# Recurrence of a four-layer hybrid network: both chunks' corrections and the inverse applied ahead of the chain, inverses in blocks of 64, and a scheduler with other prices

## The chip, the cores and the metric

The kernel runs on one core of a Trainium2 chip. Times are device microseconds of one launch; the number that counts is the median of several runs. A trace comes from one more execution, which the hardware profiler records.

## The reference, cut to what matters

A sequence of 512 tokens of width 1024 goes through four layers. Each layer is a mixer and a SwiGLU feed-forward block, each behind an RMS norm and with a residual sum. The mixers are, in this order, an RWKV-7 recurrence, sliding-window attention, a spatial gating unit and gated linear attention. The change is in the first mixer and in the scheduler that orders the whole program. The recurrence of the first mixer has 16 heads with a 64 by 64 state each:

```python
def step(state, inp):
    r_t, d_t, k_t, v_t, kk_t, a_t = inp
    sa = jnp.einsum('bhvk,bhk->bhv', state, kk_t)
    state = (state * d_t[:, :, None, :]
             - sa[..., None] * (kk_t * a_t)[:, :, None, :]
             + v_t[..., None] * k_t[:, :, None, :])
    return state, jnp.einsum('bhvk,bhk->bhv', state, r_t)
```

Its output is normalised per head (mean, variance, reciprocal root), gets a bonus term and a gate, and goes through an output projection `w_o`. All is float32.

## The kernel before

**A recorded program.** The kernel's methods do not issue instructions. Each call (`nc.tensor.matmul` and so on) is recorded as an operation with its reads and writes (`record`), a price in nanoseconds (`price`) and a latency; `Program.run` then lists them. At each turn it takes, over all engines, the operation that could start earliest by the prices, within a window of 700 operations and within the buffers of each pool; an operation that stands earlier in the program is preferred if it would start no more than `SLACK` later than the best. So the order in every engine's queue, in the feed-forward blocks too, follows from the prices. Nearly every instruction has line 233 in the profile, the line at which `run` calls it. Where the planner sees that TensorE would do too little in a stretch of time, `keep_warm` adds dummy products of the identity with itself (line 453 in the profile, `ps<-ident`): their result is not used.

**The recurrence** (`rwkv`) handles the 16 heads as four groups (`n` = 0 to 3) of two head pairs (`i`), and the 512 tokens as 8 chunks of 64, two to a block `b` of 128 tokens. For a group, `ahead(n)` does what needs no state:

- `rwkv_prepare` makes the decayed operands `qk` and `kb` (tiles `h` for even groups, `qk` for odd ones): VectorE scans, exponentials on ScalarE and products on VectorE and GpSimd.
- `rwkv_products` multiplies `kb` with `qk` (TensorE, 64 rows, 128 columns, the two heads of a pair in turn on the two halves of the rows) and masks the result into eight tiles `pa` or `pr`. ScalarE copies the part for the inverse into `z`, one buffer of 16 blocks of 128 by 128 with zeros outside two 64 by 64 blocks on the diagonal.
- `rwkv_inverse` inverts the unit triangular 64 by 64 matrices: blocks of 16 by a substitution of 15 dependent steps on VectorE (tiles `et`), then two levels of doubling on TensorE, four sets `k` of four 128 by 128 blocks each. A level is four transposes, four products with `z`, a masking copy on VectorE (`mt`), four more products and a sum. The result is in four tiles `iv`.

`rwkv_chain` walks over the 8 chunks of a group with the state `st`. One step is: state times `qk` and the correction from the other half of the block (64 by 64 products with `pa` or `pr`) into one bank, a ScalarE copy to `wu`, the 64 by 64 products with the inverse `iv`, a ScalarE copy to `vu`, the products `tok` by `vu`, and on VectorE a product and a sum with the decayed old state (which GpSimd prepares). The chunk's output is four more products per chunk and a copy to `out`. After every second block `rwkv_out` does the normalisation: two reductions and a reciprocal root on VectorE, whose small operations of 128 by 8 elements are `gmean`, `gvar`, `grs` and `rs_t`.

The program stands in the order ahead(0), the value projection, ahead(1), chain(0), ahead(2), chain(1), ahead(3), chain(2), chain(3), then the projection `w_o` for six of the eight operand tiles (`et,rk` on TensorE). Chains of different groups do not depend on each other; what comes next only waits for buffers.

## Time and profile before

| | before |
|---|---|
| median of 3 runs | 2628.28 us (2622.98 to 2630.27) |
| profiled execution, its own time | 2641.05 us |
| its span, first to last instruction | 2639.3 us |
| TensorE busy | 2554.7 us, 97% of the span |
| VectorE, ScalarE, GpSimd busy | 1853.8, 1331.6, 466.0 us |
| mean granted TensorE clock | 0.982 |

The profiled execution is 12.8 us over the median. In the profile, PE is TensorE's matmul stream, PEld its weight loads, DVE VectorE, ACT ScalarE, POOL GpSimd. Names such as `ps<-mt,z` say that a bank `ps` was written from tiles `mt` and `z`, without buffer numbers. A float32 product leaves two matmul records in the trace, a transpose or a float32r product one; so 192 records of `ps<-mt,z` are 96 products. Busy time of matmuls counts their pipeline too, so a group's busy time is more than what it delays others by.

### The profile page before, as it was taken

What the parts mean: (1) busy time and instruction counts of PE and PEld (TensorE: products, weight loads), DVE (VectorE), ACT (ScalarE), POOL (GpSimd) and SP (SyncE); (2) the same over time, 40 slices, a digit from 0 to 9 for tenths busy, and PEclk for the clock granted to TensorE, in tenths of its full rate; (3) what the DMA queues carried; (4) which work ended last, traced back from release to release, by engine and by line L of the source; (5) the groups of instructions that cost most, each with busy time, mean ns of one, the idle gap of its engine ahead of it and who ended that gap; (6) DMA issues with size and microseconds to landing.
All of it is one profiled execution on the core that took longest, in us unless ns stands there. A gap on an engine that the chain in (4) does not pass through costs nothing.

```text
span 2639.3 us, 34990 instructions
## 1 busy us (share of the span) xinstructions
PE 2554.7 (97%) x12974; PEld 2083.4 (79%) x12974; DVE 1853.8 (70%) x2888; ACT 1331.6 (50%) x2208; POOL 466.0 (18%) x492
## 2 busy tenths in 40 slices
PE   8999889999999999999999999999999999999998
PEld 7667767889888775888787888898878777888886
DVE  8675777568787966676868474478777735577868
ACT  3544343356555655655555342365645633555545
POOL 1013333311212234121112000012121000012111
PEclk8989989999999999999999999999999999999999
DMA  3220001148988622499896222379897321389885
GB/s 126 72 68 9 7 7 37 39 126 219 226 215 213 178 84 50 101 223 229 208 227 185 96 96 88 80 176 224 211 228 170 119 96 50 81 221 223 209 209 125
DMA packets 127146, 366.24 MB, mean 139 GB/s; under 512 B 13424, under 2 KB 20976, under 8 KB 126976
## 3 DMA queue, kind: packets, MB, share of 16 engines
q0 software_dynamic: 41472, 138.43, 29.1%
q1 hardware_dynamic: 85504, 225.59, 25.3%
q8 instruction: 102, 1.67, 0.3%
q14 instruction: 68, 0.56, 0.1%
HBM read 359.51 MB, written 2.10 MB: 137 GB/s over the span
## 4 chain that ended last, share of the span: by engine, by line
PE 47%; DMA 5%; issue 5%; DVE 5%; ACT 2%; POOL 0%; SPq 0%; ACTq 0%; POOLq 0%; DVEq 0%
PE ps L233 47%; DMA wraw<-ffn_o_a 2%; DMA wraw<-ffn_w_b 2%; DVE slot L233 2%; DVE wlo L233 1%; ACT whi L233 1%; DVE left L233 1%; DMA wraw<-ffn_w_a 1%; ACT slot L233 1%; POOL wraw L233 0%; DVE h L233 0%; DVE mx L233 0%; DMA wraw<-ffn_o_b 0%; DMA slot<-sg_b_s 0%; DMA slot<-slot 0%
## 5 line engine op out<-in xcount | busy, mean ns | idle before, releaser
L233 PE MATMUL ps<-whi,slot 128*128 128x512 f32 (+1 forms) x5072 | 1548.3, 383 | 14.1 <-DVE slot L233 10.0
L233 PEld LDWEIGHTS ps<-whi,slot 128*128 128x128 f32 x5072 | 942.3, 188 | 190.2 <-issue 22.7
L233 DVE TENSOR_TENSOR wlo<-wraw,whi 128x1024 fp32r<-128x1024 f32 (+2 forms) x628 | 723.1, 1157 | 421.7 <-ACT whi L233 420.5
L233 ACT CAST whi<-wraw 128x1024 fp32r<-128x1024 f32 (+3 forms) x632 | 626.6, 995 | 695.5 <-PE ps L233 528.5
L233 PE MATMUL ps<-wlo,slot 128*128 128x512 f32 (+1 forms) x2536 | 969.3, 382 | 3.7 <-DVE wlo L233 3.6
L233 PEld LDWEIGHTS ps<-wlo,slot 128*128 128x128 f32 x2536 | 476.6, 188 | 87.4 <-DVE wlo L233 7.5
L233 PE MATMUL ps<-slot,whi 128*128 128x512 f32 (+2 forms) x864 | 275.0, 396 | 1.2 <-ACT slot L233 0.9
L233 POOL DMA_DIRECT2D wraw<-ffn_w_a x128 | 109.5, 857 | 502.7 <-DVE wlo L233 363.0
L233 DVE TENSOR_TENSOR slot<-ps,slot 128x512 f32<-128x512 f32 (+2 forms) x287 | 153.3, 566 | 60.4 <-PE ps L233 45.7
L233 PEld LDWEIGHTS ps<-slot,whi 128*128 128x128 f32 (+2 forms) x864 | 156.7, 184 | 48.6 <-issue 9.1
L233 POOL DMA_DIRECT2D wraw<-ffn_w_b x64 | 54.8, 864 | 744.6 <-DMA wraw<-ffn_w_b 505.8
L233 PE MATMUL ps<-slot,wlo 128*128 128x512 f32 (+2 forms) x432 | 169.7, 393 | 0.3 <-DVE wlo L233 0.3
L233 DVE TENSOR_TENSOR slot<-left,slot 128x512 fp32r<-128x512 f32 (+1 forms) x214 | 138.9, 666 | 34.9 <-ACT slot L233 29.1
L233 DVE TENSOR_TENSOR h<-h,ps 128x512 f32<-128x512 f32 x192 | 126.7, 682 | 26.4 <-PE ps L233 25.9
L233 ACT CAST slot<-left 128x512 fp32r<-128x512 f32 (+1 forms) x214 | 124.1, 606 | 31.8 <-PE ps L233 24.7
L233 POOL DMA_DIRECT2D wraw<-ffn_o_a x64 | 54.7, 854 | 278.4 <-DVE wlo L233 162.5
L233 ACT COPY slot<-ps 128x512 f32<-128x512 f32 (+2 forms) x137 | 76.1, 568 | 52.1 <-PE ps L233 51.8
L233 PEld LDWEIGHTS ps<-slot,wlo 128*128 128x128 f32 (+2 forms) x432 | 79.5, 184 | 21.2 <-DVE wlo L233 2.2
L233 PEld LDWEIGHTS ps<-ident,slot 128*128 128x128 f32 x580 | 68.3, 142 | 34.5 <-issue 9.5
L233 PE MATMUL ps<-ident,slot 128*128 128x128 f32 x580 | 89.6, 277 | 3.3 <-POOL slot L233 2.6
L233 ACT COPY left<-ps 128x512 f32<-128x512 f32 x100 | 50.6, 556 | 63.7 <-PE ps L233 63.7
L233 DVE TENSOR_TENSOR slot<-slot 128x512 fp32r<-128x512 f32 (+9 forms) x93 | 61.5, 666 | 18.5 <-ACT slot L233 17.1
(260 smaller groups left out, 2517.3 us busy)
## 6 DMA issues: line engine op xcount, KB each, us to landing
wraw<-ffn_w_a SPq DMA_DIRECT2D x128, 512.0 KB, 6.6
wraw<-ffn_w_a POOLq DMA_DIRECT2D x128, 512.0 KB, 6.0
wraw<-ffn_o_a SPq DMA_DIRECT2D x64, 512.0 KB, 4.8
wraw<-ffn_o_a POOLq DMA_DIRECT2D x64, 512.0 KB, 7.5
wraw<-ffn_w_b SPq DMA_DIRECT2D x64, 384.0 KB, 3.5
wraw<-ffn_w_b POOLq DMA_DIRECT2D x64, 384.0 KB, 6.5
wraw<-ffn_o_b SPq DMA_DIRECT2D x16, 512.0 KB, 5.5
wraw<-ffn_o_b POOLq DMA_DIRECT2D x16, 512.0 KB, 6.1
```

Of the source, the lines that this page charges most:

```text
L233: op = self.add(eng.name, lambda: getattr(eng.target, what)(*map(real, args), **{k: real(a) for k, a in kw.items()}), *self.price(eng.name ...
```

## The change

1. **Chain.** The corrections of both chunks of a block and the products with the inverse are done for the whole block, before the steps, into the bank `xb`; a step then only adds state times `qk`. What the inverse did to `qk` in a step is done once per group by the new `rwkv_direct`: transposes of `qk`, 64 by 64 products with `iv`, and copies back into `qk`. The old state comes into the new one through a product of the identity with `st` in the bank `pb`, in place of a product on GpSimd and a sum on VectorE.
2. **Inverse.** The tiles `pa` and `pr` become one of 4096 columns per group, and the inverse reads its blocks there; `z` and the copies into it go. The sets are two of eight pairs of 64 by 64 blocks, one of each pair in the upper rows and one in the lower, in turn; the transposes there become products with a 64 by 64 piece of the identity.
3. **Normalisation.** The small scalings and the reciprocal root of `rwkv_out` go from VectorE to GpSimd (`rsqrt8`), except for its first operation.
4. **Scheduler.** Prices and latencies change for TensorE, VectorE, ScalarE and GpSimd; a change of the tile size on TensorE is priced at 92 ns, and a 64-row operation after one on the other half of the rows at 0.56 of its price; `SLACK` goes from 60 to 100. `keep_warm` now fills every planned gap of 450 ns or more up to 150 ns before its end, in place of filling up to an activity goal. This holds for the whole program.
5. **Pools.** `et` has 12 buffers for 6, `iv` 4 for 8, and some others one more or less.

```diff
-EARLY = (("pa", 8), ("iv", 8), ("ew", 3))
-LATE = (("qk", 4), ("pr", 8), ("et", 6), ("mt", 6), ("tok", 3), ("wu", 1), ("vu", 3), ("st", 5), ("out", 3), ("gn", 2))
+EARLY = (("pa", 1), ("iv", 4), ("ew", 3))
+LATE = (("qk", 4), ("pr", 1), ("et", 12), ("mt", 6), ("tok", 4), ("wu", 2), ("vu", 4), ("st", 4), ("out", 4), ("gn", 2))
...
-            return max(n * 1.667 + 5.0, m * 1.667, 340.0 if n < 16 and m == P else 0.0), 200.0
+            return max(n * 1.72 + 5.0, m * 1.72, 340.0 if n < 16 and m == P else 0.0), 200.0
...
+                if op.form[:2] != self.form[:2]:
+                    cost += self.TURN
+                elif op.form[0] == 64 and op.form[2] != self.form[2]:
+                    cost *= 0.56
...
+        if not first.done or not free or s - now < self.GAP:
+            return now
+        t = max(now, min(free) + self.SEM)
+        while True:
+            c = 224.0 if work.get(int(t // self.TICK) - 1, 0.0) >= self.BUSY else 448.0
+            if t + c > s - self.TAIL:
+                return now
             call()
...
-        for k in range(4):
-            zk = [z[:, (k * 4 + j) * P:(k * 4 + j + 1) * P] for j in range(4)]
+        halves = [(slice(0, 64), j) for j in range(8)], [(slice(64, P), j) for j in range(8)]
+        blocks = [x for pair in zip(*halves) for x in pair]
+        part = lambda t, r, j: t[r, j * 64:(j + 1) * 64]
+        for k in range(2):
+            zk = lambda r, j: z[r, k * 2048 + j * 256 + (64 if r.start else P):][:, :64]
...
+    def rwkv_direct(self, sb):
...
+        for i in range(2):
+            ps = [self.bank() for _ in range(2)]
+            for bb in range(2):
+                kt, tp = self.part("mt"), self.bank()
+                for j in range(4):
+                    t = (bb * 4 + j) * P
+                    nc.tensor.transpose(tp[:, j * P:(j + 1) * P], sb['qk'][i][:, t:t + P], self.ident)
+                nc.scalar.copy(kt, tp)
+                for b in range(2):
+                    for h in range(2):
+                        for c, ru in ((0, slice(64, P)), (1, slice(0, 64))):
+                            o, j = (b * 2 + c) * P + h * 64, i * 4 + h * 2 + b
+                            nc.tensor.matmul(ps[c][h * 64:(h + 1) * 64, (bb * 2 + b) * 64:(bb * 2 + b + 1) * 64], kt[ru, o:o + 64],
+                                             sb['inv'][bb][ru, j * 64:(j + 1) * 64], start=True, stop=True)
...
+            ab, xb = self.bank(), self.bank()
+            for i, h in heads:
+                for c, (rv, ru) in enumerate(halves):
+                    mm(ab[ru, hc(i, h)], pc(i, h, c, 1 - c)[rv], sb['v'][b][rv, hc(i, h)], start=i + h == 0, stop=True)
+            w1 = self.part("wu", w=W)
+            nc.scalar.copy(w1, ab[:, :W])
+            for i, h in heads:
+                for c, (rv, ru) in enumerate(halves):
+                    mm(xb[:, c * W:(c + 1) * W][ru, hc(i, h)], inv(i, h)[ru], w1[ru, hc(i, h)], start=i + h == 0, stop=False)
...
-                    if st is not None:
-                        nc.vector.tensor_add(ns, ns, sp)
+                        for i in range(G):
+                            mm(pb[:, col(i)], self.ident, st[:, col(i)], start=i == 0, stop=False)
...
-        nc.vector.tensor_scalar(var, var, 1.0 / 64, 64e-5, op0=ALU.mult, op1=ALU.add)
-        self.rsqrt(rs, var)
+        nc.gpsimd.tensor_mul(var, var, self.k8['mean'])
+        nc.gpsimd.tensor_add(var, var, self.k8['eps'])
+        self.rsqrt8(rs, var)
```

Three places show what this does to TensorE's queue. The first is the inverse of one group (tiles `mt`) as its first doubling level starts, with steps of another group's chain between. Before:

```order
L453 MATMUL ps<-ident 128x128 x10
L233 MATMUL ps<-ident,mt 128x128 x4
L233 MATMUL ps<-mt,z 128x128 x4
L233 MATMUL ps<-st,qk 128x128
L233 MATMUL ps<-ident,mt 128x128 x4
L233 MATMUL ps<-st,qk 128x128
L233 MATMUL ps<-mt 128x128 x4
L233 MATMUL ps<-vu,pr 64x64 x4
```

Now, in the last group:

```order
L448 MATMUL ps<-ident 128x128 x54
L233 MATMUL ps<-st,ident 128x128 x2
L233 MATMUL ps<-st,h 128x128 x2
L448 MATMUL ps<-ident 128x128
L233 MATMUL ps<-ident,mt 64x64 x16
L233 MATMUL ps<-vu,tok 128x128
L233 MATMUL ps<-mt,pr 64x64 x16
```

Runs of four operations of 128 by 128 have become runs of sixteen of 64 by 64, and the dummy products (`ps<-ident` with line 448) stand in one long run ahead of them.

The second place is a step of the chain of an odd group on TensorE, from one `st,qk` (state times `qk`) to the next. Before, with the next group's products (`qk`) between:

```order
L233 MATMUL ps<-st,qk 128x128 x2
L233 MATMUL ps<-vu,pr 64x64 x4
L233 MATMUL ps<-qk 128x128 x3
L233 MATMUL ps<-wu,iv 64x64 x4
L233 MATMUL ps<-qk 128x128 x3
L233 MATMUL ps<-vu,tok 128x128 x2
L233 MATMUL ps<-vu,pr 64x64 x4
```

Now:

```order
L233 MATMUL ps<-st,ident 128x128 x2
L233 MATMUL ps<-st,qk 128x128 x2
L233 MATMUL ps<-g_1282,tg 128x256
L233 MATMUL ps<-wu,iv 64x64
L233 MATMUL ps<-vu,tok 128x128 x2
L233 MATMUL ps<-vu,pr 64x64 x4
```

Between the state's product and `vu,tok` no 64 by 64 product of the same step is left (the `wu,iv` is one for a later block); the product `st,ident` is new.

The third place is the middle of the last feed-forward block, where TensorE multiplies split weights (`whi`, `wlo`) with split operands (`slot`). Before:

```order
L233 MATMUL ps<-wlo,slot 128x512
L233 MATMUL ps<-whi,slot 128x512 x3
L233 MATMUL ps<-wlo,slot 128x512
L233 MATMUL ps<-whi,slot 128x512 x2
L233 MATMUL ps<-wlo,slot 128x512
```

Now:

```order
L233 MATMUL ps<-wlo,slot 128x512
L233 MATMUL ps<-whi,slot 128x512 x5
L448 MATMUL ps<-ident 128x128 x12
L233 MATMUL ps<-wlo,slot 128x512
L233 MATMUL ps<-whi,slot 128x512 x2
```

The products are the same; twelve dummy products now stand between two of them. In the whole program there are 399 dummy products for 160: 62 for 35 before the recurrence, 142 for 98 in it up to the last group's outputs, and 195 for 27 behind it.

More of the change, by code (lines that the diff above doesn't have):

```diff
@@ L178 @@
 class Op:
-    __slots__ = ("i", "eng", "call", "deps", "outs", "wait", "cost", "lat", "table", "bufs", "ready", "end", "done", "columns")
+    __slots__ = ("i", "eng", "call", "deps", "outs", "wait", "cost", "lat", "table", "bufs", "ready", "end", "done", "columns", "form")
 class Engine:
@@ L298, in run @@
         dma, table, work = 0.0, None, {}
-        self.work, self.near = work, {}
+        self.work = work
         avail = {e: [] for e in now}
@@ L1261, in rwkv_chain @@
[L1261 to L1268 removed]
+                        mm(x[:, col(i)], sb['qk'][i][:, col(b * 2 + c)], st[:, col(i)], start=False, stop=False)
@@ L1319, in rwkv_out, with rsqrt8 @@
             self.split(ps[:, i * W:(i + 1) * W], sb['oo'][i][0][:, hf * W:(hf + 1) * W], sb['oo'][i][1][:, hf * W:(hf + 1) * W])
+    def rsqrt8(self, y, x):
+        nc = self.nc
+        t = self.sm.tile([P, 8], F32, name="rs8")
+        nc.vector.tensor_scalar(y.bitcast(I32), x.bitcast(I32), -0.5, float(0x5f3759df), op0=ALU.mult, op1=ALU.add)
+        nc.gpsimd.tensor_mul(x, x, self.k8['half'])
+        for _ in range(3):
+            nc.gpsimd.tensor_mul(t, y, y)
+            nc.gpsimd.tensor_mul(t, t, x)
+            nc.gpsimd.tensor_add(t, t, self.k8['one5'])
+            nc.gpsimd.tensor_mul(y, y, t)
     def row(self, ap, n=S):
```

166 lines of the change are left out of this document (73 added, 93 removed).

## The prediction

> **What bounds the kernel now.** I read the page first, then the busy times by stage, then who waits for whom on TensorE, then the groups of the recurrence's stretch.
>
> ```profile
> PE 2554.7 (97%) x12974; PEld 2083.4 (79%) x12974; DVE 1853.8 (70%) x2888; ACT 1331.6 (50%) x2208; POOL 466.0 (18%) x492
> 0.00:132.00 132.00, 123.03 (x513) 90.31 (x514) 99.75 (x162) 64.25 (x96) 10.74 (x11) 0.95 0.29 99
> 132.00:553.00 421.00, 384.23 (x2760) 317.22 (x2760) 291.50 (x569) 174.39 (x362) 131.65 (x128) 0.91 0.09 30
> 553.00:2640.00 2087.00, 2047.40 (x9704) 1675.86 (x9702) 1462.53 (x2159) 1092.97 (x1751) 323.58 (x354) 1.00 0.65 163
> ```
>
> After each stretch stand the busy microseconds of PE, PEld, DVE, ACT and POOL, then the granted TensorE clock. PE is busy for 97% of the span, so it bounds everything. But the recurrence, 132 to 553, is the one stretch where PE is not only busy: its clock averages 0.91, and the records of dummy products stand there most densely:
>
> ```profile
> 132.00:553.00 421.00, 35.84 (x196) 27.98 (x196) 0.91 0.09 30
> 553.00:2640.00 2087.00, 8.10 (x54) 7.89 (x54) 1.00 0.65 163
> ```
>
> These are the records of the dummies alone: 98 dummies in the recurrence, 27 behind it. The clock is either full or half here, so 0.91 of 421 us means about 76 us at half speed, which cost up to 38 us. Where it happens shows finer:
>
> ```profile
> 157.00:177.60 20.60, 19.84 (x80) 12.85 (x81) 10.25 (x15) 5.02 (x15) 1.32 (x1) 0.50 0.08 26
> 256.00:300.00 44.00, 36.37 (x240) 30.13 (x240) 34.99 (x72) 12.99 (x29) 18.46 (x17) 0.77 0.04 10
> 350.00:390.00 40.00, 34.13 (x212) 29.45 (x213) 28.33 (x58) 14.47 (x27) 18.78 (x18) 0.70 0.03 7
> 430.00:460.00 30.00, 24.95 (x189) 21.67 (x189) 27.41 (x56) 9.46 (x22) 17.41 (x17) 0.90 0.20 67
> ```
>
> From 157 to 177.6 PE was busy 19.84 of 20.6 us, all at half clock: about 10 us lost there alone. The other three are the times in which VectorE makes the next group's operands and substitutions; from 430 to 460 it is busy 27.41 of 30. Who PE waits for in the recurrence says the same:
>
> ```profile
> PE ps L233 <- DVE et L233: 9.9, 6, 3.5
> PE ps L233 <- DVE mt L233: 8.6, 4, 4.4
> PE ps L233 <- POOL mt L233: 3.9, 4, 2.5
> PE ps L233 <- DVE h L233: 3.7, 1, 3.7
> ...
> PE ps L233 <- DVE st L233: 1.2, 1, 1.2
> PE ps L233 <- ACT wu L233: 1.1, 3, 0.6
> ...
> PE ps L233 <- ACT vu L233: 0.5, 1, 0.5
> ```
>
> All 13 rows of that answer add up to 35.6 us. The chain's own links (`st`, `wu`, `vu`) are 2.8 of it; 26.1 belong to what runs ahead of the chain (`et`, `mt`, `h`). So a shorter step is worth little by itself; a lighter VectorE and a shorter inverse are worth more.
>
> **The change part by part.** *TensorE's work.* Prices come from back-to-back runs:
>
> ```profile
> 306.81 0.61 PE L233 MATMUL ps<-mt,z 128*128 128x128 f32 x4
> 307.26 0.61 PE L233 MATMUL ps<-mt 128*128 128x128 f32 x4
> ...
> 439.98 0.67 PE L233 MATMUL ps<-wu,iv 64*64 64x64 f32 x8
> ...
> 440.59 0.71 PE L453 MATMUL ps<-ident 128*128 128x128 f32 x4
> ...
> 246.58 2.05 PE L233 MATMUL ps<-qk 64*128 64x128 f32 x24
> 249.35 1.16 PE L233 MATMUL ps<-qk 64*128 64x128 f32 x8 [0.72 <-DVE pr L233]
> ```
>
> Two products of 128 by 128 (4 records) take 307.26 - 306.81 = 0.45 us, 0.225 each; a transpose, one record, about 0.11. Four 64 by 64 products (8 records) take 440.59 - 439.98 = 0.61 us with a change of the tile size at each end; without those changes (about 0.07 us each) 0.12 each. Taken away: 256 products and 128 transposes of the inverse, 57.6 + 14.1 = 71.7 us. Added: 48 products `st,ident`, 10.8 us, 64 transposes in the new direct form, 7.0 us, and 1152 products of 64 by 64 for 256. What one of those costs is the open price. The last two rows bound it: they are the products of `kb` and `qk`, 64 rows each, the first run mostly on the two row halves in turn, the second on one half. Four products took 1.16 us, 0.29 each; of the 12 in the first run the last four stand on one half too, so the first eight took at most 2.05 - 1.16 = 0.89 us, 0.11 each, half of a full product's 0.225. In the new order nearly all 64 by 64 products stand in turn on the two halves. At half price (0.06) the 1152 cost 69.1 us, at full price 138.2, against 30.7 for the 256: net with the rest -15.5 us or +53.6. I take **-12**, near the first, for the row with alternating halves is the nearest one, and some products stay alone.
>
> That the change counts on such pairs is where a rule speaks against it. The Trainium skill, "TensorEngine Tiling (Array Packing)", Restrictions and Gotchas, says under Gotcha 1 that different row tiles cannot access the same PSUM bank at once. In the `qk` rows the two heads go to two banks; the new pairs go to one bank, on different partitions. No run here shows 64-row pairs in one bank; by that rule the sum would take the +53.6.
>
> *The clock.* Up to 38 us were lost. The new filler puts dummies into every planned gap of 450 ns, 142 in the recurrence for 98, 13 of them ahead of the first group's operands, where the 10 us above were lost. Ends: 0 and -38; I take **-22**, the losses where PE was busy most (10 us at 157, most of the 12 from 350 to 390, where 0.70 of 40 us is 24 at half).
>
> *The waits ahead of the chain.* VectorE loses, by these rows:
>
> ```profile
> L233 DVE TENSOR_TENSOR mt<-ps,mk 128x512 f32<-128x512 f32 x24 | 16.5, 688 | 15.7 <-PE ps L233 15.4
> L233 DVE TENSOR_TENSOR st<-st 128x256 f32<-128x256 f32 x24 | 13.1, 545 | 0.4
> L233 DVE SCALAR_TENSOR_TENSOR rs_t<-gvar,rs_t 128x8 f32<-128x8 f32 x24 | 6.5, 271 | 0.6
> L233 POOL TENSOR_TENSOR mt<-et,mk 128x512 f32<-128x512 f32 x12 | 20.4, 1730 | 4.8 <-DVE rs_t L233 3.8 <-DVE gmean L233 1.1
> L233 POOL TENSOR_TENSOR st<-st,pend 128x256 f32<-128x256 f32 x24 | 16.7, 695 | 16.8 <-DVE st L233 9.9 <-PE ps L233 4.8 <-DVE rs_t L233 1.6
> ```
>
> Half of the inverse's 64 masks and sums, 32 x 0.688 = 22 us; the 24 sums into the state, 13.1; 88 small operations of the normalisation at about 0.27, 24: together 59 of its 291.5 us. GpSimd loses 24 products with the old state, 16.7 us, and half of 16 masks at 1.73, 13.8; it gains 128 operations of 128 by 8. No row has such an operation on GpSimd. The nearest are its 128x256 at 0.695 us from above, at most 89 us, and nothing from below. The cost grows with the elements (1.73 for 512 with the same kind), so I take 0.15 each, 19 us: GpSimd's 131.65 us of 421 leave room. What queues behind them is `out<-out,gn` and the masks `mt`, which TensorE waited 3.9 us for. The ends for the waits: -36 us if all go, +10 if none goes and the 44 more dummies (44 x 0.225) stand on top. I take **-16**: the substitution of 15 dependent steps stays and the shorter chain leaves PE less to do beside it; this is what is late next, and where the run of 54 dummies stands.
>
> *Behind the recurrence.* Nothing is computed otherwise, but 195 dummies stand there for 27: 168 x 0.225 = 37.8 us. They cost nothing where PE waits anyway. How much it waits there:
>
> ```profile
> PE ps L233 <- DVE slot L233: 15.0, 28, 1.5
> PE ps L233 <- DVE h L233: 5.6, 7, 1.7
> ...
> PE ps L233 <- DVE rcol L233: 0.9, 2, 0.6
> ```
>
> The seven rows add up to 28.4 us, so at least 9 us are not covered, and at most 38. At the place of the last feed-forward block that gets 12 dummies PE does not wait at all:
>
> ```profile
> 2605.57 0.84 PE L233 MATMUL ps<-whi,slot 128*128 128x512 f32 x3
> 2606.25 0.39 PE L233 MATMUL ps<-wlo,slot 128*128 128x512 f32 x1
> ```
>
> The next product starts 0.68 us after three at 0.227. I take **+22**, a bit under the middle of the two ends, for the attention stage's waits are at places with dummies. The 27 more at the start stand where PE waits for the first loads: nothing, hidden by that wait, at worst 6 us.
>
> *The sum.* -12 - 22 - 16 + 22 = -28 us. The profiled execution took 2641.05 us, 12.8 over the median of 2628.28; I take the difference over: **2600 us**.
>
> **The rivals.** *More comes free* (2566): the waits go as VectorE's 59 us would allow and most dummies behind the recurrence fall into waits: -15 - 30 - 29 + 12 = -62. For it speaks how closely PE's waits follow VectorE; against it, that the substitution is a chain.
>
> *The pairs do not overlap* (2666): the 64 by 64 products of one bank run one after the other. Then the first term is +53.6, and the rest stays: +53.6 - 22 - 16 + 22 = +38 us, slower. The place is the inverse, 768 of the products; it decides from about 0.084 us each on (28 us over 1152 above 0.06). Against it are the eight `qk` products at 0.11; for it, that those wrote two banks. This is the rule named above, as a mechanism of this kernel.
>
> *Waits become dummies* (2632): the substitution of the next group bounds the recurrence as before, so PE's waits are only filled, and all dummies behind it delay real work: -12 - 22 + 0 + 38 = +4 us. This is also the case in which the change does not do what it says: steps get shorter, but no step was waited for. For it speak the 2.8 us of the chain's links; against it, VectorE's lighter load.
>
> **How the numbers follow.** My forecast 0.50, more comes free 0.17, no overlap 0.18, waits become dummies 0.15. The forecast's own range is 2578 to 2622; with the rivals I give 2562 to 2660, which leaves out the far halves of two of them. About 0.3%, 8 us, is what a measurement of this kernel can tell from no change. Faster (under 2620.4): 0.46 of the forecast's half and the 0.17, 0.63. Within: 0.03 and 0.10, 0.13. Slower: 0.18 of the no-overlap case, 0.05 of the dummies and 0.01, 0.24.
>
> **What would show it.** In the new profile, a run of 16 products `ps<-mt` of 64 by 64 takes about 1.1 us with its tail where the pairs overlap, 2 us where not. The clock of the recurrence is above 0.96. The recurrence (from the first `twa` product to the last `ident,out`) is about 50 us shorter than 421. Behind it, PE's waits are smaller and the stretch is about 22 us longer than 2087. VectorE's busy time falls by about 59 us. I am wrong if the 64 by 64 runs take full price, if the new stretch behind grows by 35 us or more, or if PE's waits for `mt` and `et` are as long as before.

## The result: 1% slower

| | before | changed |
|---|---|---|
| median | 2626.46 us (4 runs, 2622.98 to 2630.27) | 2652.23 us (4 runs, 2650.05 to 2656.64) |
| ratio | | 1.0100, 95% interval 1.0078 to 1.0121 |
| profiled execution | 2641.05 us | 2654.14 us |
| TensorE, VectorE, GpSimd busy | 2554.7, 1853.8, 466.0 us | 2591.7, 1816.0, 454.9 us |

The forecast was 2600 us. The time lies inside the range, but on the other side of no change. The page's first line of the changed kernel already warns against reading busy time as progress, for TensorE is busier by 37 us:

```profile
PE 2591.7 (98%) x14764; PEld 2130.5 (80%) x14764; DVE 1816.0 (68%) x2744; ACT 1317.6 (50%) x2143; POOL 454.9 (17%) x591
```

The first profile of before was an unlucky execution, 15 us over its median. A second one of the same kernel took 2626.73 us, and it is the one to compare with. The stage windows of the changed kernel follow, cut where the recurrence's last output has been split (`rk`, 537.2 us), then the same two stretches for the dummies alone:

```profile
132.00:537.20 405.20, 376.99 (x4168) 313.36 (x4167) 239.68 (x429) 153.34 (x299) 130.78 (x228) 0.91 0.12 39
537.20:2652.40 2115.20, 2088.91 (x10028) 1722.66 (x10027) 1473.80 (x2156) 1100.13 (x1748) 313.42 (x351) 1.00 0.65 160
```

```profile
132.00:537.20 405.20, 37.28 (x284) 34.94 (x284) 0.91 0.12 39
537.20:2652.40 2115.20, 60.35 (x390) 54.79 (x390) 1.00 0.65 160
```

And the second profile of before, cut at the same operation (544.5 us):

```profile
132.00:544.50 412.50, 374.83 (x2794) 312.14 (x2793) 293.94 (x573) 175.95 (x365) 132.87 (x128) 0.95 0.10 33
544.50:2625.00 2080.50, 2043.66 (x9671) 1672.60 (x9669) 1460.35 (x2156) 1090.74 (x1748) 322.28 (x353) 1.00 0.66 163
```

The recurrence gained 7.3 us where about 50 were forecast. The stretch behind it lost 34.7 us where 22 were. Together that is +27.4, the difference of the two spans. (Some 3 us of each only changed sides: float32r products that stood in the recurrence before and stand outside it now.)

To see what the gap between two windows is made of, each matmul's time to the next one's start was split: up to its own length at full clock it is work, what half speed adds to that is clock, and the rest is a gap (short up to 0.35 us, a wait above). Behind the recurrence, some 12 us after the last product are in no row. Sums in microseconds:

| | recurrence, before | changed | behind, before | changed |
|---|---|---|---|---|
| other float32 products and transposes | 165.9 | 115.1 | 158.8 | 159.3 |
| products of 64 by 64 | 29.8 | 68.3 | | |
| float32r products | 83.0 | 79.6 | 1803.6 | 1806.2 |
| dummies | 21.6 | 31.5 | 5.8 | 41.1 |
| half clock | 15.1 | 27.4 | 0.7 | 3.1 |
| short gaps | 56.0 | 52.6 | 69.6 | 78.6 |
| waits | 41.1 | 30.8 | 30.7 | 14.7 |

Two things stand out. In the recurrence, waits and dummies together are 62.7 us before and 62.3 after: what left the waits went into dummies. Behind it, they went from 36.5 to 55.8. The waits of TensorE as the trace names them, first in the recurrence (all 11 rows: 27.7 us against 36.5 in the second profile of before), then behind it:

```profile
PE ps L233 <- DVE out L233: 8.1, 5, 2.6
PE ps L233 <- DVE iv L233: 4.7, 2, 2.8
PE ps L233 <- DVE h L233: 3.5, 2, 2.6
PE ps L448 <- DVE st L233: 3.2, 2, 2.3
PE ps L233 <- DVE mt L233: 3.1, 2, 2.5
```

```profile
PE ps L233 <- DVE slot L233: 6.7, 23, 1.2
PE ps L233 <- ACT slot L233: 2.4, 3, 1.3
PE ps L233 <- ACT whi L233: 1.6, 3, 0.7
```

Behind the recurrence the row for `slot` has gone from 12.8 us in the second profile of before (15.0 in the first) to 6.7 while the stretch became longer. A shorter wait is no gain when a dummy stands in its place.

### The profile page after: what moved, and what is told of

The parts are those of the page before. It is cut to its first block, busy times and chain, and to the rows that moved or that the text cites. A ratio compares the mean times of both kernels' runs of the same rounds, so it can differ in the third digit from the quotient of the medians.

```text
span 2652.4 us, 38408 instructions
## 1 busy us (share of the span) xinstructions
PE 2591.7 (98%) x14764; PEld 2130.5 (80%) x14764; DVE 1816.0 (68%) x2744; ACT 1317.6 (50%) x2143; POOL 454.9 (17%) x591
## 4 chain that ended last, share of the span: by engine, by line
PE 69%; DMA 4%; issue 4%; DVE 2%; ACT 1%; POOL 1%; ACTq 0%; POOLq 0%; DVEq 0%
PE ps L233 67%; PE ps L448 2%; DMA wraw<-ffn_o_a 1%; DMA wraw<-ffn_w_a 1%; DVE slot L233 1%; ACT whi L233 1%; DMA wraw<-ffn_w_b 1%; DVE wlo L233 1%; POOL wraw L233 0%; DMA wraw<-ffn_o_b 0%; DVE mx L233 0%; ACT slot L233 0%; POOL out L233 0%; DVE h L233 0%; POOL rs L233 0%
## 5 line engine op out<-in xcount | busy, mean ns | idle before, releaser
L233 ACT CAST whi<-wraw 128x1024 fp32r<-128x1024 f32 (+2 forms) x632 | 626.0, 993 | 739.0 <-PE ps L233 570.7
L233 DVE TENSOR_TENSOR h<-h,ps 128x512 f32<-128x512 f32 x192 | 128.4, 684 | 30.8 <-PE ps L233 29.1
L233 DVE TENSOR_TENSOR slot<-left,slot 128x512 fp32r<-128x512 f32 x214 | 136.4, 656 | 13.9 <-ACT slot L233 9.5
L448 PE MATMUL ps<-ident 128*128 128x128 f32 x798 | 115.5, 291 | 7.0 <-DVE st L233 3.2
L448 PEld LDWEIGHTS ps<-ident 128*128 128x128 f32 x798 | 107.3, 197 | 16.6 <-PE ps L448 4.9
L233 ACT COPY slot<-ps 128x512 f32<-128x512 f32 (+1 forms) x137 | 75.5, 561 | 80.6 <-PE ps L233 79.6
L233 PEld LDWEIGHTS ps<-ident,slot 128*128 128x128 f32 (+1 forms) x676 | 70.6, 141 | 25.3 <-issue 7.5
L233 PE MATMUL ps<-ident,slot 128*128 128x128 f32 (+1 forms) x676 | 88.2, 265 | 1.0 <-DVE slot L233 1.0
```

The source lines that it names most:

```text
L233: op = self.add(eng.name, lambda: getattr(eng.target, what)(*map(real, args), **{k: real(a) for k, a in kw.items()}), *self.price(eng.name ...
L448: self.nc.tensor.target.matmul(self.ps.tile_pool.tile([P, S], F32, name="ps")[:, :P], self.ident.real(), self.ident.real(), start=True, st ...
```

## The experiments

Eighteen runs followed. "Ratio" is to the kernel before, run beside each on the same chip; the changed kernel is 1.0100. The kernel before stood at medians of 2624 to 2628 us there, so medians of two rows can differ by some 4 us for that alone; the ratios do not have this error.

| run | median us | ratio, interval |
|---|---|---|
| no dummies behind | 2650.21 | 1.0095 (1.0070 to 1.0119) |
| old scheduler behind | 2620.23 | 0.9984 (0.9967 to 1.0001) |
| old prices of three engines behind | 2636.86 | 1.0035 (1.0013 to 1.0057) |
| old scheduler behind, slack 100 | 2621.19 | 0.9977 (0.9959 to 0.9995) |
| the same with TensorE's new prices behind | 2640.65 | 1.0046 (1.0027 to 1.0064) |
| old filler everywhere | 2664.53 | 1.0141 (1.0119 to 1.0164) |
| new scheduler alone | 2683.48 | 1.0227 (1.0201 to 1.0254) |
| new recurrence alone | 2652.01 | 1.0095 (1.0064 to 1.0126) |
| before, again | 2626.73 | (one run) |
| 3 of 15 steps | 2628.51 | 1.0014 (1.0000 to 1.0028) |
| tile in two halves | 2655.66 | 1.0124 (1.0107 to 1.0141) |
| old scheduler behind, dummies in the first wait | 2616.89 | 0.9965 (0.9943 to 0.9987) |
| old scheduler behind, root on VectorE | 2604.64 | 0.9921 (0.9894 to 0.9948) |
| both of these | 2597.87 | 0.9876 (0.9839 to 0.9914) |
| root on VectorE alone | 2635.66 | 1.0028 (1.0011 to 1.0045) |
| old prices of three engines everywhere | 2626.56 | 1.0004 (0.9988 to 1.0021) |
| old scheduler behind, root on VectorE, old prices | 2612.78 | 0.9941 (0.9917 to 0.9966) |
| pairs apart | 2729.33 | 1.0383 (1.0350 to 1.0416) |

### Behind the recurrence: the dummies, or the order?

The first theory was the forecast's own: dummies delay real work. The first run takes them out behind the recurrence.

```diff
-            if e == "PE" and self.warm and op.ready > 0.0:
+            if e == "PE" and self.warm and op.ready > 0.0 and op.i < self.stop:
...
+        nc.stop = len(nc.ops)
         self.load_h()
         self.rwkv_out_proj(oo, 0, 6)
```

> The changed kernel with no dummy products behind the recurrence (195 go; the 62 at the start and the 142 in the recurrence stay). Theory A, dummies delay real work: the stretch behind the recurrence grew by 33 us (from 2082 to 2115), and 195 dummies by 0.225 us are 44 us; without them most of the 33 come back, about 2652 - 30 = 2622 us. Rival B, the new prices put the products there in a worse order and the dummies only fill waits: the time stays within 8 us of 2652, and TensorE's waits behind the recurrence rise by the dummies' time.

Measured 2650.21 us: nothing came back. Theory A fell. This is where TensorE waited behind the recurrence, without a dummy there:

```profile
PE ps L233 <- DVE wlo L233: 15.6, 19, 2.2
PE ps L233 <- DVE slot L233: 12.3, 20, 1.8
PE ps L233 <- POOL slot L233: 5.7, 2, 3.1
PE ps L233 <- DVE h L233: 4.9, 3, 2.5
```

By the split above the waits rose to 53.9 us, in the place of 41.1 of dummies and 14.7 of waits; half clock took 13.5 for 3.1. The dummies had stood in waits that the order itself makes. Those are not the waits of before: `wlo` was 3.1 us in its second profile. So the order was next, by giving the operations behind the recurrence the old prices, slack and filler.

```diff
+        op = self.add(..., *(self.price_old if self.stop else self.price)(eng.name, what, args, kw))
...
+                    if floor is None or s < floor - (60.0 if op.i >= self.stop else self.SLACK):
...
+                now["PE"] = (self.keep_warm_old if op.i >= self.stop else self.keep_warm)(now["PE"], s, work)
...
+                if op.i >= self.stop:
+                    pass
+                elif op.form[:2] != self.form[:2]:
```

> The changed kernel, in which prices, slack and filler go back to those of before for every operation recorded behind the recurrence; the recurrence is scheduled as in the change. Theory D (the new prices put the products behind the recurrence in an order with more waiting, and dummies only fill that): the 22 us that the program lost behind its first 660 us come back, about 2630 us. Rival (the loss behind has another cause, such as the recurrence handing over later loads): within 8 us of 2652.

Measured 2620.23 us: 32 us came back, the whole loss and a little more. Three runs divide it. In the first only VectorE's, ScalarE's and GpSimd's prices go back:

```diff
+        op = self.add(..., *(self.price_old if self.stop and eng.name != "PE" else self.price)(eng.name, what, args, kw))
```

> The changed kernel, in which only the prices of VectorE, ScalarE and GpSimd go back to those of before for operations behind the recurrence; the slack of 100, TensorE's new prices and the new filler stay. 34 dummies are left behind the recurrence for 195. Theory P (the new prices book an operation's duration, 0.685 us of a VectorE sum of 128 by 512, where back to back they start every 0.602 us; the planner sees waits that are none and orders the products by them): the 30 us behind come back, 2618 to 2628 us. Rival (the slack or the filler did it): 2640 us or more.

Measured 2636.86: about half (15 us). The second has the old scheduler behind, as in the run before last, but keeps the new slack; its edit is shown against that run:

```diff
-                    if floor is None or s < floor - (60.0 if op.i >= self.stop else self.SLACK):
+                    if floor is None or s < floor - self.SLACK:
```

> The kernel with the old scheduler behind the recurrence (2620 us), but with the slack of 100 there in place of 60; prices and filler behind stay those of before. Old prices alone behind brought back 15 of 32 us (2637). If the slack is the other half: 2632 to 2640 us. If it is TensorE's price of a tile-size turn or the filler: 2620 us within 5.

Measured 2621.19: the slack costs nothing. The third adds TensorE's new prices to that:

```diff
-        op = self.add(..., *(self.price_old if self.stop else self.price)(eng.name, what, args, kw))
+        op = self.add(..., *(self.price_old if self.stop and eng.name != "PE" else self.price)(eng.name, what, args, kw))
...
-                if op.i >= self.stop:
-                    pass
-                elif op.form[:2] != self.form[:2]:
+                if op.form[:2] != self.form[:2]:
```

> The kernel with old prices and filler and a slack of 100 behind the recurrence (2621 us), but with TensorE's new prices there: 1.72 ns per column, 92 ns for a change of the tile size, 0.56 for a second product of 64 rows. 60 dummies behind for 31. If these prices are the half of the loss behind that the prices of the other engines left (2637 with the new filler): 2630 to 2640 us. If not, 2621 us within 5, and what is left lies with the new filler's places.

Measured 2640.65, 19 us over the run before it, with intervals far apart. So both sets of prices cost, 15 to 19 us each, in a stretch in which nothing is computed otherwise. From the old scheduler behind to the new one, the five medians form a ladder: the slack adds 1 us (2620 to 2621), TensorE's prices 19 (2641), the new filler takes 4 off (2637), and the prices of the other three engines add 15 (2652). The slack and the filler are within the error, so the two sets of prices make up the loss. Which of TensorE's three prices does it was not tried.

Why prices that look better make a worse order can be read in part. The new ones are close to what a record of the trace lasts: 681 ns for a VectorE operation on two inputs (TENSOR_TENSOR) of 128 by 512, 584 ns for a ScalarE copy of that size out of a bank. The changed kernel's group row for a sum of that kind has a mean of 684 ns, but of two in a row the second does not wait that long; the next two rows are two such operations and two copies back to back:

```profile
L233 DVE TENSOR_TENSOR h<-h,ps 128x512 f32<-128x512 f32 x192 | 128.4, 684 | 30.8 <-PE ps L233 29.1
```

```profile
583.23 1.28 DVE L233 TENSOR_TENSOR slot<-left,slot 128x512 fp32r<-128x512 f32 x2
```

```profile
694.81 1.07 ACT L233 COPY left<-ps 128x512 f32<-128x512 f32 x2 [1.97 <-PE ps L233]
```

The two operations take 1.28 us, so the second starts 1.28 - 0.68 = 0.60 us after the first; the old price is 601 ns. Two copies take 1.07, with 0.59 for one they start 0.48 apart; the old price is 476 ns. The old prices are the time an operation keeps its engine, with the rest as latency; the new ones book the whole duration as time in use. That this is how the planner comes to waits that are none is argued; that these prices cost 15 us behind the recurrence is shown.

The old filler under the new prices shows the other side:

```diff
-        if not first.done or not free or s - now < self.GAP:
-            return now
-        t = max(now, min(free) + self.SEM)
...
+        t, free = max(now, s - 2 * self.TICK), pool.slots["ps"].free
+        goal = self.LEVEL * self.BUSY / self.PARTS
```

> The changed kernel with the filler of before (up to an activity goal), everything else as changed: 34 dummies at the start, 83 in the recurrence for 142, 134 behind it for 195. Theory A: 61 fewer behind and 59 fewer in the recurrence, 27 us at 0.225 us each, of which a part was filled waiting: 2627 to 2640 us. Theory B: 2652 within 8 us. If the new filler's dummies in the recurrence had kept the clock up, its share at half speed (71.6 us in both traces) would rise here.

Measured 2664.53, slower than both theories said. Fewer dummies (251 for 399) were worse: with these prices the waits are there, and unfilled they cost some clock too. The times at half speed in the recurrence are 78.5 us for 70.5, and half clock cost 8.5 us behind it for 3.1.

### The recurrence and the scheduler, each alone

For the scheduler alone, the class that lists the operations was taken over into the kernel before, and nothing else; for the recurrence alone, the reverse.

```diff
-            return 68.0 + n * (0.52 if fast else 1.042) + 61.0 * columns, 130.0
+            return 148.0 + n * (0.52 if fast else 2.1 if what == "tensor_tensor_scan" else 1.042) + 61.0 * columns, 60.0
...
```

> The kernel before with the new scheduler alone (prices, slack, tile-size turn, new filler); recurrence as before. 419 dummies for 160: 170 behind the recurrence for 33, 187 in it for 92. Theory A: 137 more behind at 0.225 us are 31 us, most of it uncovered, and 95 more in the recurrence (21 us) partly: about 2626 + 25 to 45 = 2650 to 2670 us. Rival C, the loss comes from the recurrence's new form: about 2626 us.

```diff
-                if op.form[:2] != self.form[:2]:
-                    cost += self.TURN
-                elif op.form[0] == 64 and op.form[2] != self.form[2]:
-                    cost *= 0.56
...
```

> The new recurrence, inverse, normalisation and pools with the scheduler of before (old prices, slack 60, old filler). 28 dummies behind the recurrence, 155 in it, and 400 changes of the tile size on TensorE in the recurrence for 264. Theory A: nothing is lost behind; the recurrence keeps the 20 us that it gained, less some 12 us for the changes of the tile size (136 by about 0.09 us): 2606 to 2618 us. Rival C: 2640 us or more. If the new prices are what makes the new recurrence pay, it comes out at 2626 or above by a longer recurrence.

The scheduler alone took 2683.48 us, worse than either theory's range (waits and dummies in its recurrence, split as above, are 80.7 us for 62.7); the recurrence alone 2652.01, as bad as both together. The two parts need each other: with the new scheduler in the recurrence and the old one behind it, the same recurrence stood at 2620. The trace of the recurrence alone shows short gaps of 72.8 us there for 52.6, and waits and dummies of 73.4 for 62.3, though 13 us of float32r products moved out of it. TensorE's price of a tile-size change, without which the new recurrence has 399 such changes for 264, may be what it lacks. That price was not tried by itself, neither here nor behind the recurrence.

### Before once more, and the clock

> The kernel before, unchanged, for a second profile: the first profiled execution took 2641.05 us, 15 us over the median of its runs (2626). If that came from the clock's windows in the recurrence, this profile shows less than the 71.6 us at half speed there and its recurrence is shorter than 425 us; the new recurrence then gained less than the 20 us that the two profiles show. If not, both stretches are within 5 us of the first profile's.

It took 2626.73 us with the same code. The recurrence was 412.5 us for 425.1, and the stretch behind 2080.5 for 2082.2; the times at half speed in the recurrence sum to 37.5 us for 71.7. Nearly all of the difference is the clock: half speed cost 26.5 us of the first and 15.1 of the second, and some 7 of these 11 us lie in one place. This is 156 to 186 us of the changed kernel, of the second profile of before, and of the kernel below with dummies in the first wait:

```profile
156.00:186.00 30.00, 26.45 (x106) 19.23 (x106) 18.47 (x33) 6.31 (x9) 2.61 (x2) 0.60 0.05 18
```

```profile
156.00:186.00 30.00, 28.50 (x149) 21.01 (x150) 25.25 (x50) 12.38 (x27) 2.04 (x2) 0.94 0.20 65
```

```profile
156.00:186.00 30.00, 29.04 (x169) 21.70 (x168) 25.67 (x54) 12.15 (x18) 1.26 (x1) 1.00 0.06 19
```

TensorE works at 0.60 of its clock here in the changed kernel, behind a wait of 2.58 us for VectorE's operands:

```profile
155.74 0.33 PE L233 MATMUL ps<-ident,h 128*128 128x128 f32 x1
158.65 0.90 PE L233 MATMUL ps<-h 64*128 64x128 f32 x6 [2.58 <-DVE h L233]
```

The filler put five dummies at 150 us and none here: the plan had no gap at this place that it could fill. The next kernel puts twelve in by hand.

```diff
+            if op is self.lead and self.warm[0].slots["ps"].free:
+                for _ in range(12):
+                    self.warm[1]()
+                    self.fills += 1
             op.call()
```

> The kernel with the old scheduler behind the recurrence (2620 us), and 12 dummy products put by hand ahead of the first group's products of 64 rows, into the 2.6 us for which TensorE waits for VectorE there. In the changed kernel and all its variants with the new prices a stretch of 20 to 24 us at half clock begins right behind that wait (at 157 to 162 us). Theory K (the wait makes the clock fall): the stretch shrinks to under 7 us and the time falls by 7 to 12 us, to 2608 to 2613 us. Rival (the products of 64 rows themselves are too little activity): the clock falls all the same, 2620 us or, with 2.7 us of dummies, up to 3 more.

```profile
154.42 2.84 PE L511 MATMUL ps<-ident 128*128 128x128 f32 x24
157.20 0.93 PE L234 MATMUL ps<-h 64*128 64x128 f32 x6
```

In its profile the clock stayed full here, and half speed cost the recurrence 14.5 us for 25.6 in the kernel without these dummies. The same holds for the one other kernel that has them (the last one of the next section). Of the eighteen profiles in which TensorE waits here unfilled, 2.57 to 3.72 us, fifteen show 13.7 to 23.9 us at half speed right behind the wait. The other three show less: 6.8 us with the new recurrence alone, 3.4 in the second profile of before, none with the new scheduler alone. So the wait brings the half clock in most executions, not in each, and the dummies keep it away in the two profiled. Over all executions the mean granted clock agrees: 0.987 with the dummies for 0.984 without (ten each). The median, 2616.89, is 3 us lower, with overlapping intervals, so the gain in time is not settled by these runs.

### What holds the recurrence up

Dummies stand most densely in three stretches, those of the substitution's 15 steps on VectorE. The rows are of the dummies alone, in the changed kernel:

```profile
278.00:300.00 22.00, 11.41 (x84) 11.05 (x84) 1.00 0.01 1
350.00:362.00 12.00, 4.97 (x38) 4.59 (x38) 1.00 0.00 1
420.00:434.00 14.00, 11.37 (x101) 11.37 (x101) 1.00 0.44 143
```

One run cuts the steps; the other frees the masked products' tile in halves.

```diff
-        for i in range(1, 16):
+        for i in range(1, 4):
```

> The changed kernel with 3 of the 15 substitution steps on VectorE; it leaves out 12 steps of each group, about 10.8 us of dependent work per group. Theory S (TensorE waits, or is filled with dummies, for the substitution): 51 dummies in the recurrence for 142, and 25 to 40 us less: 2612 to 2627 us. Rival T (what bounds the recurrence is that the products of group n+2 need the one buffer that the chain of group n still reads): the next groups' products still start when a chain ends; the gain is at most the last two groups' parts, under 15 us: 2637 us or more.

```diff
-EARLY = (("pa", 1), ("iv", 4), ("ew", 3))
+EARLY = (("pa", 2), ("iv", 4), ("ew", 3))
...
-        if hf == 0:
-            sb['pr'] = self.part("pr" if sb['n'] % 2 else "pa", w=8 * S)
+        pr = self.part("pr" if sb['n'] % 2 else "pa", w=4 * S)
+        sb.setdefault('pr', []).append(pr)
```

> The changed kernel with the tile of masked products (4096 columns per group, one buffer) split into two tiles of 2048 with two buffers in the same space, so that half of it comes free when the chain of the group before last is half done; the substitution's first step is done in 8 pieces for 4. Theory T: the products of the third and fourth group start up to half a chain (15 to 30 us) sooner and the recurrence loses 10 to 20 us: 2632 to 2642 us. Theory S: within 8 us of 2652.

With three steps 2628.51 us, 24 us less, and 51 dummies for 142. That is what theory S said, a little short of its range: while VectorE substitutes, TensorE has too little else to do. It is not all that holds the recurrence up. Of the 26 us that the recurrence lost in this trace (379.2 for 405.2), 12 are waits and dummies, 50 us being left of 62, and 9 are half clock. The steps left out also took 36 us of work off VectorE (239.7 to 203.4), and the run cannot tell that from their length as a chain.

With two halves 2655.66, no gain, but the products did not start sooner either. The third group's first masking operation starts at 329.03 us for 325.29, the fourth's at 408.04 for 407.84. So this buffer is not what holds them, and theory T falls as far as it names the buffer. What earlier products would be worth is not shown.

The other candidate is the normalisation. VectorE's waits in the changed kernel, second row:

```profile
DVE st L233 <- PE ps L233: 31.1, 14, 3.2
DVE out L233 <- POOL grs L233: 18.0, 8, 3.5
```

VectorE stood 18.0 us for GpSimd's reciprocal root, a wait that cannot be in the kernel before, where VectorE makes the root itself. Everything behind `out` in VectorE's queue stood with it. The first half of one root on GpSimd, from the last block, and what VectorE does from the sum for the variance to the scaled output:

```profile
525.94 0.20 POOL L233 TENSOR_TENSOR gvar<-gvar,k8half 128x8 f32<-128x8 f32 x1 [0.28 <-DVE grs L233]
526.10 0.20 POOL L233 TENSOR_TENSOR rs<-grs 128x8 f32<-128x8 f32 x1
526.38 0.53 POOL L233 TENSOR_TENSOR rs<-rs,gvar 128x8 f32<-128x8 f32 x1
526.99 0.53 POOL L233 TENSOR_TENSOR rs<-rs,k8one 128x8 f32<-128x8 f32 x1
527.59 0.53 POOL L233 TENSOR_TENSOR grs<-grs,rs 128x8 f32<-128x8 f32 x1
528.20 0.20 POOL L233 TENSOR_TENSOR rs<-grs 128x8 f32<-128x8 f32 x1
```

```profile
524.41 0.69 DVE L233 TENSOR_REDUCE gvar<-out 128x8 f32<-128x512 f32 x1 [0.31 <-ACT out L233]
525.69 0.17 DVE L233 TENSOR_SCALAR grs<-gvar 128x8 int32<-128x8 int32 x1 [0.59 <-POOL gvar L233]
526.14 1.93 DVE L233 TENSOR_TENSOR et<-et 128x512 fp32r<-128x512 f32 x3 [0.28 <-PE ps L233]
530.39 0.69 DVE L233 TENSOR_TENSOR out<-out,grs 128x512 f32<-128x512 f32 x1 [2.32 <-POOL grs L233]
```

From the variance (its sum ends at 524.41 + 0.69 = 525.10) to the scaled output at 530.39 are 5.3 us. Two runs put the root and the small scalings back, one beside the old scheduler behind, one alone:

```diff
-        nc.gpsimd.tensor_mul(mean, mean, self.k8['mean'])
+        nc.vector.tensor_scalar(mean, mean, 1.0 / 64, None, op0=ALU.mult)
...
-        nc.gpsimd.tensor_mul(var, var, self.k8['mean'])
-        nc.gpsimd.tensor_add(var, var, self.k8['eps'])
-        self.rsqrt8(rs, var)
+        nc.vector.tensor_scalar(var, var, 1.0 / 64, 64e-5, op0=ALU.mult, op1=ALU.add)
+        self.rsqrt(rs, var)
```

> The kernel with the old scheduler behind the recurrence (2620 us), with the normalisation's small operations and reciprocal root back on VectorE. The trace of the change shows them at 0.20 to 0.53 us each on GpSimd, 5.3 us from the variance to the scaled output in the last block, against 3.2 on VectorE before. If they were a bottleneck on GpSimd: 3 to 8 us faster, 2612 to 2617. If VectorE's load was worth taking off: 5 to 15 us slower, 2625 to 2635 us.

> The changed kernel with one part undone: the normalisation's small operations and the reciprocal root back on VectorE; the new scheduler everywhere. If GpSimd's place for the root costs by itself what it cost beside the old scheduler (16 us): 2636 us within 6. If it was luck of the plan there: 2652 us within 6.

Measured 2604.64 and 2635.66: 16 and 17 us less than without that edit, in both settings. That is more than the 3 to 8 expected at first, and what the second run expected. TensorE shows where it comes from: in the second run's trace its waits and dummies in the recurrence are 47 us for 62, and its wait for `out` is 3.6 us for 8.1. On VectorE the same stretch of the last block is 2.3 us, from 497.35 to 499.61:

```profile
496.68 0.67 DVE L234 TENSOR_REDUCE gvar<-out 128x8 f32<-128x512 f32 x1
497.39 0.17 DVE L234 TENSOR_SCALAR gvar<-gvar 128x8 f32<-128x8 f32 x1
...
499.61 0.69 DVE L234 TENSOR_TENSOR out<-out,grs 128x512 f32<-128x512 f32 x1
```

VectorE's busy time in the recurrence is 249.5 us with the root and 238.2 without it: moving it saved 11 us of work and added 17.0 of waiting (18.0 in the changed kernel).

Two more runs ask whether the new prices of VectorE, ScalarE and GpSimd are worth having in the recurrence.

```diff
+        op = self.add(..., *(self.price_old if eng.name != "PE" else self.price)(eng.name, what, args, kw))
```

> The changed kernel with the prices of before for VectorE, ScalarE and GpSimd in the whole program; TensorE's new prices with the tile-size turn, the slack of 100 and the new filler stay. 62 dummies in the recurrence for 142, 34 behind for 195. Theory P: the recurrence gains as well, since its planned waits shrink too: 2595 to 2615 us. Rival (the new recurrence needs the new prices, as with the whole scheduler of before, which took 2652): 2630 us or more.

> Old scheduler behind the recurrence, root on VectorE, and in the recurrence too the prices of before for VectorE, ScalarE and GpSimd (TensorE's stay new): 55 dummies in the recurrence for 117. If prices that book durations as time in use cost in the recurrence as they do behind it: 2590 to 2600 us. If the recurrence wants the higher prices: 2605 us or more.

With the root on GpSimd the old prices everywhere gave 2626.56, 10 us less than with them only behind. With the root on VectorE they gave 2612.78, 8 us more than 2604.64, with overlapping intervals. Neither answer is general; this stays open.

Last, the two pieces that helped, in one kernel:

```diff
-        self.rsqrt8(rs, var)
+        self.rsqrt(rs, var)
...
+            if op is self.lead and self.warm[0].slots["ps"].free:
...
```

> Old scheduler behind the recurrence, the root back on VectorE (2605 us) and the 12 dummies ahead of the first group's products. If the clock's loss behind that wait is a gain of its own, another 5 to 12 us: 2593 to 2600 us. If run-to-run chance decides where the clock's windows fall, 2605 us within 5.

2597.87 us, the best of all: 0.9876 (0.9839 to 0.9914) of the kernel before, where the root alone has 0.9921 (0.9894 to 0.9948). These intervals overlap, so the second step of the gain is likely, not settled. In its profile the stretch at 157 us is at full clock again, and the mean clock is 0.990 over its four executions for 0.986 over six without the dummies.

### The pairs

```diff
-        blocks = [x for pair in zip(*halves) for x in pair]
+        blocks = halves[0] + halves[1]
```

> The changed kernel, in which a set's eight products on the upper rows stand ahead of the eight on the lower, not in turn: 768 products of the inverse lose their partner. A run of 16 products took 1.08 us in turn; without overlap 16 by 0.116 = 1.86 us. 48 runs by 0.78 us are 37 us of TensorE's time; the inverse waits on it step by step, so most of it shows: 2675 to 2690 us. If the planner's waiting (62 us of waits and dummies in the recurrence) takes most of it up: 2655 to 2665 us.

A run of 16 products of the inverse in the changed kernel, and with the pairs apart:

```profile
294.91 1.15 PE L233 MATMUL ps<-ident,mt 64*64 64x64 f32 x32
295.99 0.49 PE L233 MATMUL ps<-st,ident 128*128 128x128 f32 x2
```

```profile
406.84 1.90 PE L233 MATMUL ps<-ident,mt 64*64 64x64 f32 x32
408.66 0.49 PE L233 MATMUL ps<-vu,tok 128*128 128x128 f32 x2
```

The next product starts 1.08 us after the run's first one with the halves in turn, 1.82 us with them apart. The time was 2729.33 us, 77 us more than the changed kernel and well over both ranges, though 48 runs by 0.74 are 36. Of the rest, 23 us are waits and dummies in the recurrence (85.5 for 62.3) and 17 us clock: half speed cost 44.9 us there for 27.4. Some 17 of the 44.9 lie in one stretch, in which TensorE was busy at 0.51 of its clock:

```profile
316.00:365.00 49.00, 46.47 (x431) 42.09 (x432) 12.28 (x21) 6.45 (x17) 10.93 (x11) 0.51 0.01 1
```

## Why the prediction was wrong, step by step

**TensorE's work, -12: right.** The table gives 115.1 + 68.3 - 165.9 - 29.8 = -12.3 us. The products that stand in turn on the two halves cost 0.060 us (the 32 records of a run start 0.930 us apart from first to last, 31 steps of 0.030). The rival "the pairs do not overlap" is out. With the Trainium skill's rule ("TensorEngine Tiling (Array Packing)", Restrictions and Gotchas, Gotcha 1: different row tiles cannot access the same PSUM bank at once) the trace disagrees, for these pairs write one bank, on different partitions, and take 1.08 us for 16 against 1.82 apart.

**The clock, -22: wrong, with the sign.** The step that failed is "142 in the recurrence for 98, 13 of them ahead of the first group's operands, where the 10 us above were lost". Dummies go into gaps of the plan; the wait that cost the clock was not in the plan. Half speed cost 27.4 us of the recurrence after, 26.5 in the first profile of before and 15.1 in the second: nothing gained against the one, 12 us lost against the other. More executions side with the second: the mean clock is 0.983 over the four of the changed kernel and 0.989 over the seven of the kernel before that ran beside the first experiments. The first profile thus misled about what there was to gain. Its 2641.05 us were 15 over the median, 11 of them clock in the recurrence; the prediction took its -22 from that profile and set it against the median.

**The waits, -16: wrong.** They fell by 10.3 us, and dummies rose by 9.9. VectorE did get lighter in the recurrence, by 54 us (293.9 to 239.7) where 59 were forecast, but that was not what TensorE stood for. In the recurrence the rival "waits become dummies" was right, and the substitution is a part of the reason, as the run with three steps shows; that rival's other half, dummies that delay real work behind, fell with the first run. And one step of the sum had the wrong sign, "GpSimd's 131.65 us of 421 leave room" for the root. The operations were mis-sized a little (0.20 us, 0.53 beside some of VectorE's, for the 0.15 taken), but the sum counted them as GpSimd's work alone. The prediction asked what queues behind them on GpSimd, and not who waits for their result: VectorE, 18.0 us, with all that stands in its queue. Undone, the same recurrence gains 16 to 17 us of time.

**Behind the recurrence, +22: the size was low (about 32 when 2.6 us of moved products are taken out of 34.7), and the cause was wrong.** "Nothing is computed otherwise, but 195 dummies stand there for 27" priced only the dummies. Without any of them the time is the same; with the old scheduler behind it is 32 us less, and the two sets of prices make that up. The reordering by the new prices was priced at nothing, though it touches every engine's queue for 2100 us, four fifths of the program.

In sum -12.3 + 12.3 + 9.9 - 10.3 - 3.4 (short gaps) = -3.8 for the recurrence and +32 behind it, where -50 and +22 were forecast. The recurrence was not a bad idea: with the root on VectorE it takes 375.6 us for 412.5 (14 of that are float32r products that now stand outside it). What failed were two companions of it, the root on GpSimd and the prices used outside the stretch they were made for.

## What to carry to other kernels

A change to a planner's prices is a change to the whole program: price the stretch in which nothing else changes first, and undo the prices there before anything else. Filled idle time is not work found: add dummies and waits before comparing. When work moves to an engine with spare time, ask who needs the result and what stands in that engine's queue behind the wait; 18 us of waiting came from 11 us of work moved.

## What the runs showed of the hardware

- Pairs of 64 by 64 products on the two halves of the rows overlap in one bank: 0.060 us each for 0.108 apart.
- GpSimd's operations of 128 by 8 took 0.20 us alone and 0.53 us while VectorE ran operations of 128 by 512 with both inputs in SBUF (`et<-et`, 526.38 to 528.1 above). In the same trace the 17 that ran wholly beside a VectorE operation with a bank as one input took 0.20 us. The Trainium skill ("GPSIMD Engine Reference", 1. Specifications) says that the engine shares its SBUF interface with VectorE and contends with VectorE's instructions of two SBUF inputs; these rows agree.
- The same code at the same place (157 us) ran 3.4 us at half clock in one execution and 20.5 in another. One profile of such a stretch is one draw.
